# A two-layer-pair network on one core: each FFN begins with two plain column groups instead of one, and all phases share one pool of 2 KB weight tiles

## The chip, the core and the metric

The kernel runs on one core of a Trainium2 chip. Its five engines work side by side, each through its own queue in order: TensorE (PE, with its weight loads PEld), VectorE (DVE), ScalarE (ACT), GpSimd (POOL) and SyncE (SP), which here only issues transfers. The metric is device microseconds of one execution. The kernel before took 2481.24 us, the median of three runs between 2480.6 and 2482.82 us.

## The reference

A sequence of 512 positions of width 1024 goes through four layers, each a mixer and an FFN with residual additions: an mLSTM mixer, a windowed attention mixer, a parallel mixer (sparse attention beside a state-space branch) and a short convolution. All of it is float32. The part that matters here is the FFN, four times with weights of its own and D_FF = 2816:

```
def rmsnorm(x, w):
    xf = x.astype(jnp.float32)
    y = xf * lax.rsqrt(jnp.mean(xf * xf, axis=-1, keepdims=True) + EPS)
    return (y * w.astype(jnp.float32)).astype(x.dtype)

def swiglu(h, w_in, w_out):
    gu = h @ w_in
    gate, up = gu[..., :D_FF], gu[..., D_FF:]
    return (jax.nn.silu(gate) * up) @ w_out

x = x + swiglu(rmsnorm(x, norm_w), w_in, w_out)
```

## The kernel before

**Layout and arithmetic.** x lies transposed in eight tiles xT of 128 features by 512 positions. Every float32 product is made of three matmuls: each operand is split into a high part (whi, xh), which ScalarE rounds (`split`, L176; `hilo`, L232), and a low part (wlo, xl), the rest, which VectorE subtracts (`sub`, L164), and high x high, high x low and low x high are summed in one PSUM bank (`mm3`, L216 to L218). So each weight costs one pass of ScalarE and one of VectorE before TensorE can use it.

**The FFN.** The 2816 columns of gate and of up are worked through in 11 groups jj of 256 gate and 256 up columns. Group 0 is *plain* (`first`, L498): four blocks of 128 columns, 8 tiles of x each, 96 matmuls of 512 columns. The norm is folded in: the matmuls read x times the norm's weight (xh, xl from L289 and L290), and the row scale rb, which needs the sums of squares of all eight tiles (L282, L298, L255), multiplies the result when it is evacuated (L510). Groups 1 to 10 use a Strassen scheme (`seven`, L456): seven products of 24 matmuls with 256 columns, 168 in all, in the place of eight. It needs sums of weight blocks (S, L423 on GpSimd and L428 on VectorE) and four combinations of x (`combine`, L390, tiles thi and tlo). Products go to banks g, s, t and o (`seven`, L457); the third is the first that goes to t. After three or four groups the down projection adds to x (`out_part`).

**Banks.** `share` gives each tag its PSUM banks; in the FFN g has two, s three, t two and o one. The plain group asks for t, o, t, o (L505), and its norm uses s. The mixers' output projections (`add_out`, L333) use g and s, in the short convolution s and t.

**Weight buffers.** `wpool` (L1646) opens a pool for each phase: in a mixer 8 buffers of 2 KB a partition for high parts and as many for low ones, in an FFN 4 of 4 KB. With 4 KB a split covers 1024 elements a partition (4 tiles of x by 256 columns), with 2 KB 512. Raw weights come in 512 KB transfers into 5 buffers (`load_raw`, L181).

**What sets the order.** The program is written phase after phase, and a scheduler of the framework places each engine's instructions when the program is built, by the order of writing as a priority and by when it expects inputs and free buffers. In the text the first group's weights stand behind the norm.

The functions that the change touches, with what calls them:

## Time and profile before

| | before |
|---|---|
| median of three runs | 2481.24 us |
| the profiled execution | 2479.76 us, of which its span 2478.1 us |
| TensorE busy | 2388.4 us (96%), 14196 matmuls |
| VectorE busy | 1866.2 us (75%) |
| ScalarE busy | 1160.3 us (47%) |
| GpSimd busy | 437.2 us (18%) |
| granted TensorE clock, mean | 0.984 |
| read from HBM | 219.45 MB, 89 GB/s |

The granted clock is the share of 2.4 GHz that TensorE was given; it has two levels, 0.5 and 1.0 of that. A matmul's shown duration is longer than its distance to the next one, since matmuls are pipelined; how fast they run is read from their starts, or from how many fit in a stretch. The four FFNs begin at about 248, 830, 1576 and 2117 us of the span. A wait is put down to the instruction whose semaphore came last.

### The profile page before, as it was taken

The numbers are of one execution on the slowest core, as the hardware profiler recorded it, in microseconds if no ns is written. First come the engines' busy times: TensorE is split into PE (matmuls) and PEld (weight loads), VectorE is DVE, ScalarE is ACT, GpSimd is POOL, SyncE is SP. The second block draws the span as 40 slices with busy tenths as digits, with TensorE's granted clock in tenths as the row PEclk, the third lists the DMA queues.
The fourth block names the chain that finished last, engine by engine and source line by source line (L and its number), as shares of the span: only waits on it lengthen the run. The fifth ranks groups of instructions, "written<-read, shape, count | busy, mean of one in ns | idle before, by whom it ended". The sixth has DMA issues, their size and how long they took to land.

```text
span 2478.1 us, 36192 instructions
## 1 busy us (share of the span) xinstructions
PE 2388.4 (96%) x14196; PEld 2088.1 (84%) x14196; DVE 1866.2 (75%) x2826; ACT 1160.3 (47%) x1869; POOL 437.2 (18%) x318
## 2 busy tenths in 40 slices
PE   8999899999999899999999899899999999999998
PEld 7898799998767698989777777798989788899997
DVE  7677888787867786967889978876867755857777
ACT  4444544444577553534554455453534323545434
POOL 2210100000352100000456346100000010101100
PEclk9999999999989999999999999999999999999999
DMA  4331232323311132323221133222323332223232
GB/s 164 116 99 43 94 115 86 119 81 116 98 39 35 60 103 85 120 85 100 94 62 60 52 110 100 80 86 94 111 94 103 102 97 91 88 91 120 82 107 77
DMA packets 73434, 226.60 MB, mean 91 GB/s; under 512 B 10336, under 2 KB 14576, under 8 KB 73264
## 3 DMA queue, kind: packets, MB, share of 16 engines
q1 hardware_dynamic: 68896, 220.00, 26.8%
q10 hardware_dynamic: 4320, 4.21, 0.6%
q8 instruction: 111, 1.82, 0.3%
q14 instruction: 59, 0.48, 0.1%
q0 software_dynamic: 48, 0.10, 0.0%
HBM read 219.45 MB, written 2.20 MB: 89 GB/s over the span
## 4 chain that ended last, share of the span: by engine, by line
PE 82%; DVE 10%; DMA 2%; ACT 2%; issue 2%; POOL 1%; ACTq 0%; SPq 0%; DVEq 0%; POOLq 0%
PE ps_g L216 6%; PE ps_g L218 6%; PE ps_g L217 6%; PE ps_g L446 5%; PE ps_g L445 5%; PE ps_g L444 5%; PE ps_s L216 4%; PE ps_s L218 3%; PE ps_s L217 3%; PE ps_t L444 3%; PE ps_t L445 3%; PE ps_t L446 3%; PE ps_t L217 3%; PE ps_t L216 3%; PE ps_t L218 3%; DVE wlo L164 2%
## 5 line engine op out<-in xcount | busy, mean ns | idle before, releaser
L176 ACT ACTIVATE whi<-wraw 128x512 fp32r<-128x512 f32 (+1 forms) x488 | 394.7, 819 | 614.0 <-PE ps_g L217 195.8
L164 DVE TENSOR_TENSOR wlo<-wraw,whi 128x512 fp32r<-128x512 f32 (+1 forms) x428 | 441.1, 1040 | 173.2 <-ACT whi L176 164.3
L423 POOL TENSOR_TENSOR S<-wraw 128x1024 f32<-128x1024 f32 x40 | 117.0, 2924 | 1161.7 <-DMA wraw<-in_in_dram 995.1
L176 ACT ACTIVATE whi<-S 128x1024 fp32r<-128x1024 f32 x160 | 169.6, 1060 | 261.3 <-PE ps_g L445 115.5
L216 PE MATMUL ps_g<-xh,whi 128*128 128x512 f32 (+1 forms) x632 | 259.3, 410 | 14.0 <-DVE fa L1223 6.4
L164 DVE TENSOR_TENSOR wlo<-S,whi 128x1024 fp32r<-128x1024 f32 x160 | 209.2, 1308 | 76.2 <-ACT whi L176 76.2
L218 PE MATMUL ps_g<-xh,wlo 128*128 128x512 f32 (+1 forms) x632 | 254.8, 403 | 1.0 <-DVE wlo L164 1.0
L217 PE MATMUL ps_g<-xl,whi 128*128 128x512 f32 (+1 forms) x632 | 254.1, 402 | 0.0
L446 PE MATMUL ps_g<-thi,wlo 128*128 128x256 f32 x640 | 183.3, 286 | 5.5 <-DVE wlo L164 5.5
L444 PE MATMUL ps_g<-thi,whi 128*128 128x256 f32 x640 | 183.1, 286 | 3.7 <-ACT whi L176 3.7
L445 PE MATMUL ps_g<-tlo,whi 128*128 128x256 f32 x640 | 182.8, 286 | 0.0
L216 PEld LDWEIGHTS ps_g<-xh,whi 128*128 128x128 f32 (+1 forms) x632 | 121.8, 193 | 45.6 <-DVE fa L1223 7.5
L218 PEld LDWEIGHTS ps_g<-xh,wlo 128*128 128x128 f32 (+1 forms) x632 | 121.5, 192 | 29.5 <-issue 2.2
L217 PEld LDWEIGHTS ps_g<-xl,whi 128*128 128x128 f32 (+1 forms) x632 | 121.8, 193 | 25.2 <-issue 1.1
L446 PEld LDWEIGHTS ps_g<-thi,wlo 128*128 128x128 f32 x640 | 124.7, 195 | 6.3 <-DVE wlo L164 6.3
L444 PEld LDWEIGHTS ps_g<-thi,whi 128*128 128x128 f32 x640 | 124.5, 195 | 4.6 <-ACT whi L176 4.6
L445 PEld LDWEIGHTS ps_g<-tlo,whi 128*128 128x128 f32 x640 | 124.5, 195 | 0.0
L164 POOL TENSOR_TENSOR wlo<-wraw,whi 128x512 fp32r<-128x512 f32 (+1 forms) x60 | 79.6, 1336 | 142.0 <-ACT whi L176 96.2
L217 PE MATMUL ps_s<-hlo,whi 128*128 128x512 f32 x264 | 102.8, 389 | 0.0
L218 PE MATMUL ps_s<-hhi,wlo 128*128 128x512 f32 x264 | 102.7, 389 | 0.0
L216 PE MATMUL ps_t<-hhi,whi 128*128 128x512 f32 x264 | 102.7, 389 | 0.0
L217 PE MATMUL ps_t<-hlo,whi 128*128 128x512 f32 x264 | 102.7, 389 | 0.0
(564 smaller groups left out, 6980.0 us busy)
## 6 DMA issues: line engine op xcount, KB each, us to landing
wraw<-in_in_dram SPq DMA_DIRECT2D x176, 512.0 KB, 3.5
wraw<-in_down_dram SPq DMA_DIRECT2D x82, 512.0 KB, 3.5
wraw<-in_par_in_dram SPq DMA_DIRECT2D x30, 512.0 KB, 3.6
wraw<-in_mlstm_in_dram SPq DMA_DIRECT2D x24, 512.0 KB, 3.9
wraw<-in_sc_in_dram SPq DMA_DIRECT2D x24, 512.0 KB, 3.5
wraw<-in_attn_in_dram SPq DMA_DIRECT2D x12, 512.0 KB, 4.2
wraw<-in_par_out_dram SPq DMA_DIRECT2D x12, 512.0 KB, 5.9
mb<-drs SPq DMA_DIRECT2D x16, 256.0 KB, 3.6
```

The costliest lines, as they stand in the source:

```text
L164: (V if e == "V" else G).tensor_tensor(lo, x, hi.bitcast(F32), op=ALU.subtract)
L176: A.activation(hi, raw[:, k:k + st, :], AF.Copy)
L216: T.matmul(o, lhsT=w[0], rhs=x[0], start=start, stop=False)
L217: T.matmul(o, lhsT=w[0], rhs=x[1], start=False, stop=False)
L218: T.matmul(o, lhsT=w[1], rhs=x[0], start=False, stop=stop)
L423: G.tensor_tensor(live[jj, "S1"], live[jj, 2], live[jj, 3], op=ALU.add)
L444: T.matmul(o, lhsT=w[0], rhs=x[i][0], start=start and i == j == 0, stop=False, skip_group_check=True)
L445: T.matmul(o, lhsT=w[0], rhs=x[i][1], start=False, stop=False, skip_group_check=True)
L446: T.matmul(o, lhsT=w[1], rhs=x[i][0], start=False, stop=end, skip_group_check=True)
```

## The change

Each FFN now begins with two plain groups. `plain_weights` asks for a plain group's weights; the first group's stand ahead of the norm in the text, the second's behind the first group's matmuls. The first group goes to banks g, s, g, s, the second to t, o, t, o. The combinations of x are written after the first group's evacuation, and the Strassen runs begin with group 2. All phases take their weights from one pool with 8 buffers of 2 KB for high and 8 for low parts, so every split covers at most 512 elements, also in the Strassen products and in the down projections; the norm uses bank t. The gate weights of the mLSTM take their tiles from the same pool.

```
@@ -68,6 +68,7 @@
     sp = ctx.enter_context(tc.tile_pool(name="sp", bufs=2, **RIGHT))
     rp = ctx.enter_context(tc.tile_pool(name="rp", bufs=3, **RIGHT))
     xsp = ctx.enter_context(tc.tile_pool(name="xsp", bufs=8))
+    wp = ctx.enter_context(tc.tile_pool(name="wp", bufs=8))
     pp = ctx.enter_context(tc.tile_pool(name="pp", bufs=1, space=PSUM))
     dp = ctx.enter_context(tc.tile_pool(name="dp", bufs=1, space=bass.MemoryType.DRAM))
...
@@ -163,20 +165,12 @@
         e = lo_on[0][turn[0] % len(lo_on[0])]
         (V if e == "V" else G).tensor_tensor(lo, x, hi.bitcast(F32), op=ALU.subtract)
 
-    def weight_tile(tag, name, nk, n):
-        pool, bufs, _ = weight_pool
-        return pool.tile([P, nk, n], F32R, tag=tag, name=name, bufs=bufs)
-
     def split(raw, nk, n):
-
-        res = []
-        st = max(1, min(nk, weight_pool[2] // n))
-        for k in range(0, nk, st):
-            hi, lo = weight_tile("whi", "whi", st, n), weight_tile("wlo", "wlo", st, n)
-            A.activation(hi, raw[:, k:k + st, :], AF.Copy)
-            sub(lo, raw[:, k:k + st, :], hi)
-            res += [(hi[:, i, :], lo[:, i, :]) for i in range(st)]
-        return res
+        hi = wp.tile([P, nk, n], F32R, tag="whi", name="whi", bufs=WB)
+        lo = wp.tile([P, nk, n], F32R, tag="wlo", name="wlo", bufs=WB)
+        A.activation(hi, raw, AF.Copy)
+        sub(lo, raw, hi)
+        return [(hi[:, k, :], lo[:, k, :]) for k in range(nk)]
 
     def load_raw(w, k0, c0):
         rows, n, cw, mk = _W[w]
@@ -194,11 +188,6 @@
         for k in range(0, nk, 4):
             m = min(4, nk - k)
             raw = load_raw(w, k0 + k, c0)
-            if weight_pool[2] >= m * n:
-                w4 = split(raw, m, n)
-                for b in range(0, n, P):
-                    res[b // P] += [(hi[:, b:b + P], lo[:, b:b + P]) for hi, lo in w4]
-                continue
             for b in range(0, n, P):
                 res[b // P] += split(raw[:, :, b:b + P], m, P)
         return res
@@ -206,10 +195,11 @@
     def load_b(w, k0, nk, c0, n):
 
         res = []
-        mk = _W[w][3]
+        mk, st = _W[w][3], 512 // n
         for k in range(0, nk, mk):
             raw = load_raw(w, k0 + k, c0)
-            res += split(raw, mk, n)
+            for i in range(0, mk, st):
+                res += split(raw[:, i:i + st, :], st, n)
         return res
 
     def mm3(o, w, x, start, stop):
@@ -361,9 +351,20 @@
         V.tensor_tensor(xT[m], ps, xT[m], op=ALU.add)
 
 
+    def plain_weights(wi, jj):
+
+        ws = [], [], [], []
+        for k in (0, 4):
+            for n, c in enumerate((0, DFF)):
+                raw = load_raw(wi, k, c + jj * 256)
+                for i in range(2):
+                    ws[n + 2 * i].extend(split(raw[:, :, i * P:(i + 1) * P], 4, P))
+        return ws
+
     def ffn(L, last=False, aside=None):
         wi, wd = f"in{L}", f"down{L}"
-        xs = norm(f"ffn{L}", tag="s", later=True)
+        pending = plain_weights(wi, 0)
+        xs = norm(f"ffn{L}", later=True)
         parts = [(0, 3), (3, 6), (6, 9), (9, 11)] if last else [(0, 4), (4, 8), (8, 11)]
         hid = {}
         HS = slice(0, S // 2), slice(S // 2, S)
@@ -430,7 +431,7 @@
                     live[jj, "S2"] = t
             else:
                 t = {0: r[0], 1: r[1], 2: live[jj, "S1"], 6: r[3]}[s]
-            live[jj, "w", s] = split(t, 4, 256)
+            live[jj, "w", s] = [split(t[:, :, j * P:(j + 1) * P], 4, P) for j in range(2)]
 
         def product(jj, s, ps, start):
             ws = live.pop((jj, "w", s))
@@ -438,8 +439,7 @@
             for j in range(2):
                 o = ps[:, HS[j]]
                 for i in range(4):
-                    c = slice(j * P, (j + 1) * P)
-                    w = [t[:, c] for t in ws[i]]
+                    w = ws[j][i]
                     end = i == 3
                     T.matmul(o, lhsT=w[0], rhs=x[i][0], start=start and i == j == 0, stop=False, skip_group_check=True)
                     T.matmul(o, lhsT=w[0], rhs=x[i][1], start=False, stop=False, skip_group_check=True)
@@ -495,23 +495,22 @@
             for jj in jjs:
                 seven(jj, ahead)
 
-        def first():
-            ws = [], [], [], []
-            for k in (0, 4):
-                for n, c in enumerate((0, DFF)):
-                    for hi, lo in split(load_raw(wi, k, c), 4, 256):
-                        for i in range(2):
-                            ws[n + 2 * i].append([t[:, i * P:(i + 1) * P] for t in (hi, lo)])
-            pss = group_a(xs, ws, ["t", "o", "t", "o"], {4: xs.sums, 6: xs.rows})
-            for i in range(4):
-                combine(i)
+        def plain_evac(jj, pss):
             g, u = scr("fg", (P, 2, S)), scr("fu", (P, 2, S))
             for i in range(2):
                 V.tensor_tensor(g[:, i, :], pss[2 * i], xs.rb, op=ALU.mult)
             A.activation(g, g, AF.Silu)
             for i in range(2):
                 V.tensor_tensor(u[:, i, :], pss[2 * i + 1], g[:, i, :], op=ALU.mult)
-            store(0, u)
+            store(jj, u)
+
+        def first():
+            pss = group_a(xs, pending, ["g", "s", "g", "s"], {4: xs.sums, 6: xs.rows})
+            ws = plain_weights(wi, 1)
+            plain_evac(0, pss)
+            for i in range(4):
+                combine(i)
+            plain_evac(1, group_a(xs, ws, ["t", "o", "t", "o"]))
 
 
         def add_row(m, ps):
@@ -611,7 +610,7 @@
 
         first()
         for p, (a, b) in enumerate(parts):
-            run(range(max(a, 1), b))
+            run(range(max(a, 2), b))
             if last:
                 if p == 0:
                     xnat = to_nat()
...
@@ -1642,12 +1641,6 @@
     rope = ExitStack()
     TILE = dict(reuse_waits="tile")
 
-    @contextmanager
-    def wpool(name, bufs, width):
-        with tc.tile_pool(name=name, bufs=bufs, **TILE) as pool:
-            weight_pool[:] = pool, bufs, width
-            yield
-
     for n, L in enumerate(layers):
         last = n == len(layers) - 1
         if L == 1 and n == 0:
...
@@ -1668,7 +1661,7 @@
         if before_window:
             rope_pool[0] = rope.enter_context(tc.tile_pool(name="rope", bufs=1, **RIGHT))
         share(PB[4])
-        with wpool(f"wf{L}", 4, 1024), tc.tile_pool(name=f"tf{L}", bufs=4, **TILE) as hidden[1], \
+        with tc.tile_pool(name=f"tf{L}", bufs=4, **TILE) as hidden[1], \
                 tc.tile_pool(name=f"hf{L}", bufs=4, **TILE) as hidden[0], \
                 tc.tile_pool(name=f"ff{L}", bufs=2, **TILE) as phase[0]:
             ffn(L, last=last, aside=rope_tables if before_window else None)
```

In the order as built (an instruction's line is that of its own file: L164 of before is L166 now, L348 is L338, L290 is L280, L282 is L272, L510 is L501, L397 is L398) the change shows at three places, all at the beginning of FFN 0.

VectorE at the end of the mLSTM's output projection. xT is x, and its numbers are the eight tiles. Before:

```order
L348 TENSOR_TENSOR xT_106<-ps_g,xT_106 128x512
L348 TENSOR_TENSOR xT_107<-ps_s,xT_107 128x512
L348 TENSOR_TENSOR xT_108<-ps_g,xT_108 128x512
L348 TENSOR_TENSOR xT_109<-ps_s,xT_109 128x512
L290 SCALAR_TENSOR_TENSOR xl<-xT_106,cols,xh 128x512
L290 SCALAR_TENSOR_TENSOR xl<-xT_107,cols,xh 128x512
L282 TENSOR_TENSOR ssum<-ssum,sq 128x512
```

The same place now:

```order
L338 TENSOR_TENSOR xT_109<-ps_g,xT_109 128x512
L338 TENSOR_TENSOR xT_110<-ps_s,xT_110 128x512
L166 TENSOR_TENSOR wlo<-wraw,whi 128x512
L338 TENSOR_TENSOR xT_111<-ps_g,xT_111 128x512
L166 TENSOR_TENSOR wlo<-wraw,whi 128x512
L338 TENSOR_TENSOR xT_112<-ps_s,xT_112 128x512
L166 TENSOR_TENSOR wlo<-wraw,whi 128x512
L280 SCALAR_TENSOR_TENSOR xl<-xT_109,cols,xh 128x512
L166 TENSOR_TENSOR wlo<-wraw,whi 128x512
```

Low parts of weights have moved in between the residual additions, three of them ahead of the norm's first xl.

VectorE around the evacuation of the first plain group (fg and fu are its gate and up halves, S a sum of weight blocks). Before:

```order
L164 TENSOR_TENSOR wlo<-S,whi 128x1024
L510 TENSOR_TENSOR fg<-ps_t,rb 128x512 x2
L465 TENSOR_TENSOR fg<-ps_s,pc 128x2x256
L428 TENSOR_TENSOR S<-S,wraw 128x1024
L513 TENSOR_TENSOR fu<-ps_o,fg 128x512
```

And now:

```order
L166 TENSOR_TENSOR wlo<-wraw,whi 128x512 x4
L501 TENSOR_TENSOR fg<-ps_g,rb 128x512 x2
L504 TENSOR_TENSOR fu<-ps_s,fg 128x512 x2
L398 TENSOR_TENSOR fu<-S 128x512
L166 TENSOR_TENSOR wlo<-wraw,whi 128x512 x2
L400 TENSOR_TENSOR fu<-S,fu 128x256
L223 TENSOR_TENSOR hlo<-fu,hhi 128x1024
```

Before, the evacuation stands behind low parts of Strassen weights, with a Strassen product's result (L465) right after it; now it stands behind the second plain group's weights, and the first combination of x (L398) comes after it.

TensorE at the end of the first plain group. Before:

```order
L216 MATMUL ps_t<-xh,whi 128x512
L217 MATMUL ps_t<-xl,whi 128x512
L218 MATMUL ps_t<-xh,wlo 128x512
L444 MATMUL ps_g<-xh,whi 128x256
L445 MATMUL ps_g<-xl,whi 128x256
L446 MATMUL ps_g<-xh,wlo 128x256
```

And now:

```order
L206 MATMUL ps_g<-xh,whi 128x512
L207 MATMUL ps_g<-xl,whi 128x512
L208 MATMUL ps_g<-xh,wlo 128x512
L206 MATMUL ps_s<-xh,whi 128x512
L207 MATMUL ps_s<-xl,whi 128x512
L208 MATMUL ps_s<-xh,wlo 128x512
L206 MATMUL ps_t<-xh,whi 128x512
L207 MATMUL ps_t<-xl,whi 128x512
L208 MATMUL ps_t<-xh,wlo 128x512
L206 MATMUL ps_o<-xh,whi 128x512
```

Where the first Strassen product followed the plain group, the second plain group follows now, in other banks. The order of SP's transfers is the same in both but for one pair of small transfers in the parallel mixer.

## Rows read from the trace of the kernel before

**Rows 1.** the page's first part: busy time, share of the span, instructions.

```profile
PE 2388.4 (96%) x14196; PEld 2088.1 (84%) x14196; DVE 1866.2 (75%) x2826; ACT 1160.3 (47%) x1869; POOL 437.2 (18%) x318
```

**Rows 2.** windows, Strassen run and mixer: stretch, length, busy (count) by engine.

```profile
400.00:460.00 60.00, 60.00 (x503) 60.00 (x502) 53.20 (x49) 33.13 (x39) 7.11 (x2) 1.00 0.33 107
1980.00:2040.00 60.00, 60.00 (x266) 49.68 (x265) 31.13 (x48) 15.81 (x25) 5.88 (x4) 1.00 0.31 97
```

**Rows 3.** windows at the beginnings of the four FFNs, columns as above.

```profile
245.00:300.00 55.00, 46.44 (x261) 40.51 (x260) 43.90 (x63) 27.85 (x33) 9.41 (x2) 0.94 0.22 77
827.00:882.00 55.00, 47.70 (x266) 41.77 (x265) 43.46 (x64) 28.37 (x34) 9.15 (x2) 0.94 0.21 77
1573.00:1640.00 67.00, 57.12 (x335) 50.97 (x335) 57.47 (x78) 38.44 (x47) 5.82 (x2) 0.92 0.25 86
2115.00:2160.00 45.00, 42.86 (x256) 37.38 (x255) 37.97 (x50) 22.45 (x26) 7.82 (x2) 1.00 0.27 94
```

**Rows 4.** the same windows, L216's matmuls alone: length, PE busy (count), clock.

```profile
245.00:300.00 55.00, 13.96 (x36) 0.94 0.22 77
827.00:882.00 55.00, 14.14 (x36) 0.94 0.21 77
1573.00:1640.00 67.00, 14.23 (x36) 0.92 0.25 86
2115.00:2160.00 45.00, 13.66 (x35) 1.00 0.27 94
```

**Rows 5.** TensorE's waits in the whole span: us in total, times, longest.

```profile
PE ps_t L444 <- DVE fg L510: 8.3, 3, 3.7
PE ps_g L216 <- DVE fa L1223: 6.4, 3, 3.8
PE ps_g L446 <- DVE wlo L164: 5.5, 4, 3.2
PE ps_t L1042 <- ACT rd L1062: 3.9, 1, 3.9
```

**Rows 6.** TensorE's timeline in FFN 0: start, us, what [idle before <-releaser].

```profile
283.72 0.58 PE L444 MATMUL ps_t<-thi,whi 128*128 128x256 f32 x1 [3.71 <-DVE fg L510]
284.10 0.41 PE L445 MATMUL ps_t<-tlo,whi 128*128 128x256 f32 x1
284.31 0.41 PE L446 MATMUL ps_t<-thi,wlo 128*128 128x256 f32 x1
```

**Rows 7.** the chain of waits, 245 to 300 us: start, us, what.

```profile
257.98 7.07 POOL S L423
```

**Rows 8.** VectorE's timeline in a Strassen run, columns as in rows 6.

```profile
408.02 0.68 DVE L476 TENSOR_TENSOR fu<-ps_g,pc 128x512 f32<-128x512 f32 x1
408.62 0.68 DVE L478 TENSOR_TENSOR fu<-ps_o,pc 128x512 f32<-128x512 f32 x1
411.48 1.22 DVE L479 TENSOR_TENSOR fu<-fu,fg 128x1024 f32<-128x1024 f32 x1
412.62 1.22 DVE L164 TENSOR_TENSOR wlo<-S,whi 128x1024 fp32r<-128x1024 f32 x1
417.17 2.89 DVE L164 TENSOR_TENSOR wlo<-wraw,whi 128x1024 fp32r<-128x1024 f32 x1 [0.46 <-ACT whi L176]
```

**Rows 9.** timeline ahead of FFN 0: first residual addition, first FFN matmul.

```profile
235.32 0.69 DVE L348 TENSOR_TENSOR xT<-ps_g,xT 128x512 f32<-128x512 f32 x1 [1.45 <-PE ps_g L218]
248.38 0.50 PE L216 MATMUL ps_t<-xh,whi 128*128 128x512 f32 x1 [0.86 <-ACT whi L176]
```

**Rows 10.** VectorE's groups by shape: count | busy us, mean ns | idle.

```profile
L164 DVE TENSOR_TENSOR wlo<-wraw,whi 128x1024 fp32r<-128x1024 f32 x218 | 283.2, 1306 | 116.3 <-ACT whi L176 115.5
L164 DVE TENSOR_TENSOR wlo<-wraw,whi 128x512 fp32r<-128x512 f32 x210 | 158.1, 764 | 56.9 <-ACT whi L176 48.8 <-PE ps_t L255 7.2 <-PE ps_g L218 0.5
```

**Rows 11.** VectorE's waits, 400 to 460 us, columns as in rows 5.

```profile
DVE wlo L164 <- ACT whi L176: 4.6, 6, 1.7
DVE fg L471 <- PE ps_t L446: 0.9, 1, 0.9
```

More of the change, by code (lines that the diff above doesn't have):

```diff
@@ L1 @@
-from contextlib import ExitStack, contextmanager
+from contextlib import ExitStack
 import numpy as np
@@ L91, in tile_net @@
     hidden = [None, None]
-    weight_pool = [None, 0, 0]
     def hid_tile(tag, bufs, dt=F32R):
@@ L102, in scr @@
         return pool.tile(list(shape), dt, tag=tag, name=tag, bufs=bufs)
+    WB = 8
     RB = 5
@@ L638, in mlstm @@
         for k in (0, 4):
-            hi = weight_tile("whi", "ghi", 4, P)
-            lo = weight_tile("wlo", "glo", 4, P)
+            hi = wp.tile([P, 4, P], F32R, tag="whi", name="ghi", bufs=WB)
+            lo = wp.tile([P, 4, P], F32R, tag="wlo", name="glo", bufs=WB)
             G.memset(hi.bitcast(F32), 0.0)
@@ L1658, in tile_net @@
         if L == 2:
-            with wpool(f"wm{L}", 8, 512), tc.tile_pool(name=f"hm{L}", bufs=8) as hidden[0]:
+            with tc.tile_pool(name=f"hm{L}", bufs=8) as hidden[0]:
                 parallel(n > 0)
         else:
-            with wpool(f"wm{L}", 8, 512), tc.tile_pool(name=f"hm{L}", bufs=8) as hidden[0], \
+            with tc.tile_pool(name=f"hm{L}", bufs=8) as hidden[0], \
                     tc.tile_pool(name=f"mix{L}", bufs=2) as phase[0]:
```

## The prediction, made before the changed kernel ran

> **What bounds the kernel now.** I read the page's first part, then the busy time of stretches, then the waits, and only then the timeline, because a share over the whole span mixes stages with different limits. TensorE is busy 96% of the span, VectorE 75% [rows 1]. Two stretches show what TensorE costs when nothing holds it up: 503 matmuls of 256 columns in 60 us inside a Strassen run, 0.1193 us each, and 266 matmuls of 512 columns in 60 us, 0.2256 us each [rows 2]. Inside the Strassen runs and the down projections TensorE is 60.00 of 60 busy at full clock; a change there can win only by taking matmuls away.
>
> The loss is at the four places where an FFN begins. Four windows each begin with the last 12 matmuls of the mixer's output projection and end when the second Strassen group is under way [rows 3]. Of their matmuls, three times the L216 count have 512 columns [rows 4], 12 are the small ones of the norm (taken here as 0.12 us each, an estimate from the 256-column matmul), the rest have 256. FFN 0: 108 x 0.2256 + 141 x 0.1193 + 1.4 = 42.6 of 55 us, so 12.4 us lost. FFN 1: 108 and 146 make 43.2 of 55, lost 11.8. FFN 2: 108 and 215 make 51.4 of 67, lost 15.6. FFN 3: 105 and 139 make 41.7 of 45, lost 3.3. Together 43.1 us, 1.7% of the span, and it is what a change of the FFN's beginning can reach.
>
> Who ends these waits: the largest, 8.3 us in three waits, is the Strassen product into bank t that waits for L510, the evacuation of the plain group that sat in the same bank; next come waits for VectorE's low halves of the weights, 5.5 us [rows 5]. The timeline shows the rest of the price: TensorE starts at 283.72 after 3.71 us of idle time, and its matmuls then stand 0.21 us apart where 0.12 is normal [rows 6]; the granted clock of the window is 0.94 [rows 3], which is a few us at the lower of the two levels, 1.2 GHz. 24 matmuls at 0.09 us more are 2.2 us. The chain of waits in the same window runs over VectorE and a 7.07 us sum on GpSimd [rows 7], not over transfers: at an FFN's start VectorE (43.90 of 55 us busy [rows 3]) has the residual additions, the norm, all four combinations of x for Strassen, and the split weights, and the only plain group gives TensorE 21.7 us to hide them behind.
>
> **The change part by part.**
>
> *A second plain group in place of a Strassen group.* 96 x 0.2256 = 21.65 us against 168 x 0.1193 = 20.04 us [rows 2]: +1.61 us in each FFN, +6.4 us in all. This is certain, since TensorE is the bound there.
>
> *What the second group hides.* TensorE then has 43.3 us of plain work before the first Strassen product. VectorE's work in that time, at the spacing of its starts, 0.60 us for 512 elements and 1.14 for 1024 [rows 8]: 8 residual additions 4.8, 8 xl 5.3 (at 0.66, an estimate a tenth over 0.60), 7 sums of squares 4.2, 16 half-size low parts of plain weights 9.6, the norm's small ones 2.3 (estimate), evacuating the first group 2.4 and its low half 1.1, four combinations with their low halves 9.7, the first four Strassen low parts 2.4: 41.8 us. It begins, as before, 13 us ahead of the FFN's first matmul, while the projection still runs [rows 9]. So 41.8 us of VectorE stand against 56 us of TensorE, where before some 35 us (the same list without the second group's share and the first group's evacuation, which had to wait) stood against the same 13 us and 21.7. The evacuation of the first group no longer stands in the Strassen product's way, since that group lies in banks g and s and the second lies between. I therefore let the 43.1 us go, and ask what is late next: the second plain group is still evacuated from t, and the third Strassen product needs t and the fourth combination. That costs two evacuations and one low half, 2 x 0.60 + 1.14 = 2.3 us, in FFN 0 to 2 and one low half, 1.1 us, in FFN 3: 8 us left. Its bounds are 0 (all of it behind the two products into g and s, 5.8 us) and the whole wait as it is today, 8.3 us of idle time plus three stretches at the lower clock, 14.9 us more than forecast.
>
> *Weights asked for ahead of the norm.* Four low parts now stand between the residual additions on VectorE, 4 x 0.60 = 2.4 us, so the norm's first xl comes 2.4 us later; the first matmul that reads it is 13 us behind the first addition [rows 9], so I count nothing. It takes away the two waits at the first plain matmuls, already in the 43.1. All eight weight buffers may still be held by the projection; then part of those two waits, about 2 us an FFN, comes back. SP's queue keeps its order, so no transfer moves past another.
>
> *Banks g and s for the first group.* The projection has just used them, so the last of four blocks waits for the last residual addition; that addition feeds the norm's last xl anyway. I count 0, at most one addition, 0.6 us, in each FFN.
>
> *2 KB weight tiles everywhere.* A split of 1024 elements becomes two of 512: 2 x 0.60 - 1.14 = 0.06 us more on VectorE by starts [rows 8], or 2 x 0.764 - 1.306 = 0.22 us by mean durations [rows 10]. A Strassen group has 7 splits: 0.4 to 1.6 us more per 20.04 us. VectorE is busy 53.20 of 60 us there [rows 2], 17.8 us a group; 18.2 to 19.3 fit. I take the lower end, as the durations overlap their successors, and cost it at nothing: what hides it is VectorE's own idle time of 5.5 us in 60 [rows 11].
> The Trainium skill ("Perfetto Trace Analysis", section "Optimizing Scalar/DVE Operations") puts some 60 ns of access overhead on each VectorE instruction and says that larger operations help when the engine is saturated. Its figure gives the same 0.4 us a group as the starts do; by its rule the split costs time only from saturation on, which is the slower rival below, and 53.20 of 60 says not yet.
>
> *The mixers.* Their tiles and counts stay, but the scheduler interleaves the window and the parallel mixer anew. One long wait more or less in each is the bound I give it, 3.8 and 3.9 us [rows 5]: +-8 us, taken as 0.
>
> Sum on the profiled execution, whose span of 2478.1 lies in 2479.76 us: 2479.8 - 43.1 + 6.4 + 8 = 2451.1. The median of the runs, 2481.24, lies 1.5 us above it, so the forecast is 2452.5.
>
> **Rivals.** *The wait for t stays.* The second group's evacuation replaces the first's: VectorE, in order, reaches it behind combinations, and the third Strassen product is late just as now. For it: the banks t and o are the same, and o is a single bank. Against it: the row scale is long known by then, and two products lie in front. Price 14.9 us: 2467.
>
> *VectorE becomes the bound in the Strassen runs (slower).* Place: the 36 groups left. 17.8 us busy plus 1.6 by durations plus the 1.8 us a group in which VectorE waits for ScalarE's high part or a product [rows 11], if those waits stay because each half split waits again: 21.2 against 20.04, 1.1 us a group, 40 us, so 2492. It decides from 20.04 us a group on, and makes the kernel slower than before from 0.8 us over. For it: one split that started at 417.17 took 2.89 us, as if something held VectorE up [rows 8]. Against it: that one is already in the 53.20, and waits shrink when work fills them.
>
> *More goes than forecast.* Nothing is left at the FFN starts and the mixers gain a wait: 2452.5 - 8 - 4 = 2440.
>
> *The mixers give it back in part*, one long wait each plus the weight waits of the projection: 2452.5 + 8 + 6 = 2466.
>
> **How the numbers follow.** Forecast (2444 to 2460) 0.62, wait for t 0.14, mixers 0.06, more gained 0.06, VectorE the bound 0.12. The predicted time is 2452. The range of 2440 to 2474 takes in all but the slow rival and some of the edges. A change under 0.2%, 5 us, can't be told from none here. Faster 0.88; the slow rival with its lower prices gives 0.03 of no change and 0.09 of slower.
>
> **What would show it.** Right: at the four FFN starts no wait of TensorE over 3 us, a granted clock of 1.00, and 43 us of plain matmuls without a hole before the first Strassen product; 384 more 512-column matmuls and 672 fewer of 256. The half splits start 0.60 us apart and VectorE stays below 19.3 us a Strassen group. Wrong: TensorE's share below 60 of 60 inside a Strassen run with the waits put down to VectorE's low parts, or a wait of over 3 us at the third Strassen product for the second group's evacuation.

## The result and the profile after

The changed kernel takes 2452.8 us (median of 4 runs, 2451.14 to 2453.84), the kernel before 2481.6 in the same series: a ratio of 0.9883, 95% interval 0.9866 to 0.9900. The forecast was 2452. The profiled run took 2452.76 us with a span of 2451.0. The time is right and so is most of the way to it, but the step on what is late next was not, and the errors of the sum nearly cancel. One of seven executions of experiment 2 took 4782.31 us and is left out of its median below.

The page's first part, as in [rows 1]:

```profile
PE 2382.7 (97%) x13908; PEld 2072.2 (85%) x13908; DVE 1866.8 (76%) x3172; ACT 1205.6 (49%) x2219; POOL 428.0 (17%) x314
```

288 matmuls fewer: 384 more of 512 columns, 672 fewer of 256, as forecast. VectorE has 346 instructions more and the same busy time. The same four windows as [rows 3], then L206 alone (L216 before) as [rows 4], with its weight loads beside TensorE's busy time:

```profile
245.00:300.00 55.00, 53.28 (x271) 45.10 (x269) 41.80 (x72) 28.36 (x43) 2.63 (x1) 1.00 0.20 60
827.00:882.00 55.00, 53.93 (x328) 48.08 (x327) 46.34 (x71) 28.77 (x43) 5.13 (x2) 1.00 0.24 77
1573.00:1640.00 67.00, 63.49 (x386) 56.80 (x385) 53.54 (x83) 34.34 (x51) 5.61 (x2) 0.95 0.26 79
2115.00:2160.00 45.00, 45.00 (x279) 40.64 (x278) 40.09 (x58) 26.24 (x39) 2.46 (x1) 1.00 0.35 106
...
245.00:300.00 55.00, 24.79 (x64) 11.90 (x64) 1.00 0.20 60
```

Before, TensorE was busy 46.44, 47.70, 57.12 and 42.86 us in these windows [rows 3]. The clock is now 1.00 in three windows and 0.95 in FFN 2. By the count of the prediction FFN 0 now does 192 x 0.2256 + 67 x 0.1193 + 1.4 = 52.7 us of work in 55; 12.4 us were lost there, 2.3 are now.

The largest waits of TensorE in the span, as in [rows 5]; the wait for t behind L510 (now L501) is gone from the list, the mixers' remain:

```profile
PE ps_g L206 <- DVE fa L1222: 5.4, 3, 4.7
PE ps_s L155 <- POOL ident masks.py:199: 5.0, 1, 5.0
PE ps_t L245 <- DVE nrc L298: 4.4, 1, 4.4
PE ps_s L943 <- issue: 3.9, 1, 3.9
```

What is left stands in FFN 2. Its TensorE timeline (start, length, what, idle time before):

```profile
1603.96 0.28 PE L445 MATMUL ps_t<-tlo,whi 128*128 128x256 f32 x1
1604.92 0.39 PE L446 MATMUL ps_t<-thi,wlo 128*128 128x256 f32 x1 [0.68 <-DVE wlo L166]
...
1607.71 0.58 PE L444 MATMUL ps_g<-thi,whi 128*128 128x256 f32 x1 [1.92 <-ACT whi L171]
...
1608.72 0.58 PE L445 MATMUL ps_t<-tlo,whi 128*128 128x256 f32 x1 [0.21 <-DVE tlo L223]
...
1610.15 0.58 PE L444 MATMUL ps_t<-thi,whi 128*128 128x256 f32 x1 [0.63 <-ACT thi L222]
...
1611.18 0.41 PE L444 MATMUL ps_g<-thi,whi 128*128 128x256 f32 x1
1611.39 0.41 PE L445 MATMUL ps_g<-tlo,whi 128*128 128x256 f32 x1
```

TensorE waits for halves of weights and of combinations, 3.4 us in all and not for an evacuation, and its matmuls then stand 0.21 us apart where 0.12 is normal: the lower of the two clock levels, as in FFN 0 before [rows 6].

To compare kernels I use one measure from the timelines: the time from an FFN's first matmul to the first matmul of its down projection. With two plain groups and two Strassen groups it is 192 x 0.2256 + 336 x 0.1193 = 83.4 us of work, and the shortest measured is 85.2 (FFN 3, with one Strassen group: 65.1); with one plain group 1.6 less. "Lost" is the sum of what lies above these, worked out from the rounded figures and good to some 0.2 us. In experiment 2, 24 projection matmuls that are mixed into FFN 0 and FFN 1 are taken out (5.4 us each) and counted with the mixers. "Mixers" is the time from the program's start, or the last matmul of an FFN, to the next FFN's first matmul, summed over the four. Experiment 8 changes the Strassen groups themselves and has no row.

| kernel | ratio to before | FFN 0, 1, 2, 3 (us) | lost | mixers |
|---|---|---|---|---|
| before | 1 | 95.2, 94.3, 97.5, 66.9 | 39.7 | 1048.0 |
| after | 0.9883 | 87.7, 87.1, 92.5, 65.2 | 11.8 | 1042.2 |
| 1 one group | 1.0159 | 105.5, 102.5, 104.0, 81.8 | 79.6 | 1050.9 |
| 2 first group in t, o | 0.9966 | 92.3, 92.3, 92.2, 66.1 | 22.2 | 1048.2 |
| 3 combinations first | 0.9839 | 85.2, 85.2, 85.2, 65.1 | 0 | 1037.1 |
| 4 three groups in FFN 2 | 0.9879 | 87.8, 87.1, 88.1, 65.2 | 5.9 | 1042.6 |
| 5 = 3 with one group | 0.9936 | 91.3, 91.4, 97.6, 63.4 | 29.5 | 1039.7 |
| 6 before, 2 KB tiles | 1.0029 | 90.1, 90.2, 95.3, 68.0 | 29.4 | 1066.9 |
| 7 before, second group | 1.0019 | 95.1, 94.2, 97.1, 70.2 | 35.9 | 1049.9 |
| 9 before, group and banks | 0.9894 | 86.6, 86.1, 86.7, 65.5 | 4.2 | 1051.3 |
| 10 = 3 again | 0.9828 | 85.2, 85.2, 85.2, 65.1 | 0 | 1037.3 |
| 11 = 3, FFN 3 with one group | 0.9820 | 85.2, 85.2, 85.2, 63.4 | 0 | 1044.2 |
| 12 = 3, pools by phase | 0.9894 | 86.1, 86.1, 86.6, 65.9 | 4.0 | 1054.9 |

Before to after: 39.7 - 11.8 = 27.9 us no longer lost, 6.4 paid for dearer matmuls, 5.8 gained in the mixers: 27.3, against 27.1 between the spans.

Every row of the table is one execution. The FFN segments repeat: FFN 0, 1 and 2 are 85.2 us each in experiments 3, 10 and 11, and FFN 0, 1 and 3 agree within 0.1 us between the changed kernel and experiment 4. The mixers do not: experiments 10 and 11 have the same instructions up to FFN 3, and their mixers differ by 6.9 us. So a difference of up to 7 us in that column is not shown to come from an edit. Of the 5.8 here, 3.3 are seen: before, TensorE waits 0.86, 0.92 and 1.53 us for its first weights ahead of FFN 0, 1 and 2 (the first of them in [rows 9]), and after the change it doesn't.

### The profile page after: what moved, and what is told of

It reads as the page before. It is cut to its first block, busy times and chain, and to the rows that moved or that the text cites. A ratio compares the mean times of both kernels' runs of the same rounds, so it can differ in the third digit from the quotient of the medians.

```text
span 2451.0 us, 36810 instructions
## 1 busy us (share of the span) xinstructions
PE 2382.7 (97%) x13908; PEld 2072.2 (85%) x13908; DVE 1866.8 (76%) x3172; ACT 1205.6 (49%) x2219; POOL 428.0 (17%) x314
## 4 chain that ended last, share of the span: by engine, by line
PE 61%; DVE 8%; ACT 1%; issue 1%; DMA 1%; POOL 0%; ACTq 0%; DVEq 0%
PE ps_g L206 4%; PE ps_g L207 4%; PE ps_g L208 4%; PE ps_g L446 3%; PE ps_g L444 3%; PE ps_g L445 3%; PE ps_s L206 3%; PE ps_s L208 3%; PE ps_s L207 3%; PE ps_t L207 2%; PE ps_t L206 2%; PE ps_t L208 2%; PE ps_t L446 2%; PE ps_t L445 2%; PE ps_t L444 2%; PE ps_o L446 1%
## 5 line engine op out<-in xcount | busy, mean ns | idle before, releaser
L171 ACT ACTIVATE whi<-wraw 128x512 fp32r<-128x512 f32 (+1 forms) x726 | 447.6, 621 | 670.6 <-PE ps_g L207 237.0
L166 DVE TENSOR_TENSOR wlo<-wraw,whi 128x512 fp32r<-128x512 f32 x666 | 487.8, 743 | 186.5 <-ACT whi L171 173.8
L424 POOL TENSOR_TENSOR S<-wraw 128x1024 f32<-128x1024 f32 x36 | 104.0, 2889 | 1146.8 <-DMA wraw<-in_in_dram 794.2
L206 PE MATMUL ps_g<-xh,whi 128*128 128x512 f32 (+1 forms) x696 | 283.6, 409 | 9.2 <-DVE fa L1222 5.2
L207 PE MATMUL ps_g<-xl,whi 128*128 128x512 f32 (+1 forms) x696 | 279.8, 402 | 0.0
L208 PE MATMUL ps_g<-xh,wlo 128*128 128x512 f32 (+1 forms) x696 | 279.3, 402 | 0.0
L171 ACT ACTIVATE whi<-S 128x512 fp32r<-128x512 f32 x288 | 178.1, 628 | 191.0 <-PE ps_g L445 59.0
L166 DVE TENSOR_TENSOR wlo<-S,whi 128x512 fp32r<-128x512 f32 x288 | 202.7, 730 | 35.0 <-ACT whi L171 33.2
L206 PEld LDWEIGHTS ps_g<-xh,whi 128*128 128x128 f32 (+1 forms) x696 | 134.0, 193 | 40.8 <-DVE fa L1222 5.8
L444 PE MATMUL ps_g<-thi,whi 128*128 128x256 f32 x576 | 163.8, 284 | 2.7 <-ACT whi L171 1.9
L446 PE MATMUL ps_g<-thi,wlo 128*128 128x256 f32 x576 | 163.7, 284 | 0.2
L445 PE MATMUL ps_g<-tlo,whi 128*128 128x256 f32 x576 | 163.4, 284 | 0.0
L166 POOL TENSOR_TENSOR wlo<-wraw,whi 128x512 fp32r<-128x512 f32 (+1 forms) x60 | 83.2, 1397 | 139.2 <-ACT whi L171 124.2
L206 PE MATMUL ps_t<-hhi,whi 128*128 128x512 f32 x264 | 102.7, 389 | 0.0
```

Of the source, the lines that this page charges most:

```text
L166: (V if e == "V" else G).tensor_tensor(lo, x, hi.bitcast(F32), op=ALU.subtract)
L171: A.activation(hi, raw, AF.Copy)
L206: T.matmul(o, lhsT=w[0], rhs=x[0], start=start, stop=False)
L207: T.matmul(o, lhsT=w[0], rhs=x[1], start=False, stop=False)
L208: T.matmul(o, lhsT=w[1], rhs=x[0], start=False, stop=stop)
L424: G.tensor_tensor(live[jj, "S1"], live[jj, 2], live[jj, 3], op=ALU.add)
```

## The experiments

The ratios go with the runs of the kernel before on the same chip, whose median was 2479 to 2480 us in all four series.

**1. One group.** From the changed kernel:

```diff
-            ws = plain_weights(wi, 1)
             plain_evac(0, pss)
...
-            plain_evac(1, group_a(xs, ws, ["t", "o", "t", "o"]))
...
-            run(range(max(a, 2), b))
+            run(range(max(a, 1), b))
```

> The changed kernel with the second plain group taken out again: group 0 stays in banks g and s, its weights stay ahead of the norm, the tiles stay 2 KB. Theory A (the second group is what hides VectorE's work at an FFN's start): the 6.4 us of dearer matmuls go and at least 25 of the some 31 us that the starts had gained come back, 2452.8 - 6.4 + 25 = 2471 us (2465 to 2478), with TensorE waits for VectorE ahead of the first Strassen products. Theory B (the banks and the early weights did it, the second group only costs): 2452.8 - 6.4 = 2446 us (to 2451).

Measured: 2517.3 us, ratio 1.0159 (1.0143 to 1.0175). Theory A holds in sign and is far short in size: not 25 us came back but 68 (from 11.8 lost to 79.6). TensorE's waits in its FFN 0, then VectorE's there (us in total, times, longest):

```profile
PE ps_t L444 <- ACT whi L171: 10.6, 1, 10.6
...
DVE fg L501 <- ACT rb L246: 5.5, 1, 5.5
DVE nv L288 <- PE ps_t L239: 4.3, 1, 4.3
DVE ssum L272 <- ACT sq L271: 2.6, 3, 1.2
DVE fu L504 <- ACT fg L502: 2.5, 1, 2.5
```

In these four rows VectorE waits 14.9 us of the 55 from 245 to 300 us. It is not short of time, it works in order: L501, the evacuation, waits for rb, the norm's row of scales, and everything behind it waits along. ScalarE, in order as well, shows how that reaches TensorE:

```profile
282.68 2.00 ACT L222 ACTIVATE thi<-fu 128x1024 fp32r<-128x1024 f32 x2 [2.80 <-DVE fu L401]
285.25 1.15 ACT L171 ACTIVATE whi<-S 128x512 fp32r<-128x512 f32 x2 [0.57 <-POOL S L424]
```

The high half that TensorE waits 10.6 us for comes behind high halves of combinations that waited for VectorE. That makes the order of evacuation and combinations (experiment 3) the suspect.

**2. The first group back in t and o.** From the changed kernel:

```diff
-        xs = norm(f"ffn{L}", later=True)
+        xs = norm(f"ffn{L}", tag="s", later=True)
...
-            pss = group_a(xs, pending, ["g", "s", "g", "s"], {4: xs.sums, 6: xs.rows})
+            pss = group_a(xs, pending, ["t", "o", "t", "o"], {4: xs.sums, 6: xs.rows})
```

> The changed kernel with its first plain group back in banks t and o (the norm's small sums in s, as before the change); both plain groups then use the same banks. Theory A (cover by matmuls is the main thing): only the evacuation of group 0 stands in the way of group 1, some 2.4 us of VectorE and a few matmuls at the lower clock in each FFN, 2456 to 2462 us. Theory B (banks of their own are the main thing): the 8.3 us of waits for t come back, now ahead of group 1, with half clock behind them: 2467 us or more.

Measured: 2470.9 us, ratio 0.9966 (0.9954 to 0.9977), B by the time; at the starts 10.4 us more are lost, between the two, and 6.0 us more stand in the mixers, no more than two executions of the same mixers differ by. Its TensorE in FFN 0:

```profile
265.67 1.11 PE L245 MATMUL ps_s<-ident,nrc 128*128 128x128 f32 x4 [2.66 <-DVE nrc L234]
268.20 0.79 PE L206 MATMUL ps_t<-xh,whi 128*128 128x512 f32 x1 [1.41 <-DVE fg L501]
```

The second group cannot begin before the first is out of t, and that waits for the scales (nrc). 4.1 us of idle time, and FFN 0 loses 7.1: the rest passes at the lower clock (the clock is 0.94 from 244 to 300 us).

**3. Combinations first.** From the changed kernel, the order in the text that the kernel before had:

```diff
             ws = plain_weights(wi, 1)
-            plain_evac(0, pss)
             for i in range(4):
                 combine(i)
+            plain_evac(0, pss)
```

> The changed kernel with the four combinations written ahead of the first group's evacuation, as they were before the change. Theory A: nothing needs banks g and s before the first Strassen product, 21.65 us later, and the sum of VectorE's work is the same: 2453 us (2450 to 2456). Rival: VectorE's order is what counts (the evacuation early, the combinations late), and putting it back costs a wait for g or s at the first Strassen product, 2 to 4 us in each FFN: 2460 us or more.

Measured: 2438.7 us, ratio 0.9839 (0.9822 to 0.9856); again 2437.7, 0.9828 (0.9813 to 0.9842). Both expectations are wrong: neither had a gain, and all that was left at the starts went, 11.8 us; the medians lie 14.1 us apart, the mixers of the two profiled executions 5. The interval lies below that of the change, so this version beats both kernels. VectorE in FFN 0, first in the changed kernel, then in the repeated run of this one (start, length, what, idle time before):

```profile
264.01 0.16 DVE L288 TENSOR_SCALAR nv<-ps_t 128x4 f32<-128x4 f32 x1 [4.27 <-PE ps_t L239]
...
272.45 1.29 DVE L501 TENSOR_TENSOR fg<-ps_g,rb 128x512 f32<-128x512 f32 x2 [1.29 <-ACT rb L246]
276.21 1.29 DVE L504 TENSOR_TENSOR fu<-ps_s,fg 128x512 f32<-128x512 f32 x2 [2.46 <-ACT fg L502]
277.41 0.68 DVE L398 TENSOR_TENSOR fu<-S 128x512 f32<-128x512 f32 x1
```

```profile
245.10 0.68 DVE L398 TENSOR_TENSOR fu<-S 128x512 f32<-128x512 f32 x1
...
263.83 1.22 DVE L223 TENSOR_TENSOR tlo<-fu,thi 128x1024 fp32r<-128x1024 f32 x1
270.44 0.16 DVE L288 TENSOR_SCALAR nv<-ps_t 128x4 f32<-128x4 f32 x1 [1.93 <-PE ps_t L239]
...
280.25 1.29 DVE L501 TENSOR_TENSOR fg<-ps_g,rb 128x512 f32<-128x512 f32 x2
```

Behind the evacuation the first combination starts at 277.41; ahead of it at 245.10, in the holes between the norm's steps, and the last one's low half starts at 263.83. The evacuation starts 8 us later, and nobody waits, since the second group stands in other banks. TensorE in this FFN 0 and FFN 2 (columns as in [rows 2]):

```profile
243.00:300.00 57.00, 57.00 (x297) 48.98 (x296) 51.00 (x81) 31.93 (x48) 5.11 (x2) 1.00 0.26 84
1573.00:1640.00 67.00, 67.00 (x457) 62.38 (x457) 56.91 (x81) 36.23 (x55) 5.23 (x2) 1.00 0.34 111
```

**4. A third group in FFN 2.** From the changed kernel: in FFN 2 groups in t, o, then g, s, then t, o.

```diff
+            order = [["t", "o", "t", "o"]] * three + [["g", "s", "g", "s"]]
+            for jj, banks in enumerate(order):
+                pss = group_a(xs, ws, banks, {} if jj else {4: xs.sums, 6: xs.rows})
+                ws = plain_weights(wi, jj + 1)
+                plain_evac(jj, pss)
...
+            run(range(max(a, 3 if three else 2), b))
```

> The changed kernel with a third plain group in FFN 2 alone, where 7.9 us are still lost (banks t and o, then g and s, then t and o). Theory A (VectorE's work of the FFN's start is still more than two groups hide there): the 7.9 us fall to 1 or less for 1.6 us of dearer matmuls: 2446.5 us (2444 to 2450). Rival: what is late there is the preparing of the Strassen weights itself (difference, high half, low half), which moves along with the first product: nothing gained, 1.6 us paid, 2454 us (2452 to 2457).

Measured: 2448.9 us, ratio 0.9879 (0.9862 to 0.9896). In FFN 2, 92.5 became 88.1, of which 86.8 can't be avoided with three groups: theory A, as far as the segment goes (1.3 us are left, where 1 or less was expected). The interval overlaps that of the change, so the whole time doesn't show it. It buys cover where experiment 3 needs none.

**5. Experiment 3 with one group.** The lines of experiment 1, taken out of experiment 3.

> One plain group in banks g and s, with the combinations ahead of its evacuation as in the kernel before; 2 KB tiles and weights ahead of the norm as in the changed kernel. It is the run of 2438.66 us (combinations first) without its second group. Theory A (one group hides too little of VectorE's work, in whatever order): 6.4 us of dearer matmuls go, 15 to 30 us are lost again at the four starts: 2455 us (2447 to 2462). Rival (banks of their own and the combinations first suffice, the second group only costs): 2438.7 - 6.4 = 2432 us (2430 to 2437).

Measured: 2463.9 us, ratio 0.9936 (0.9922 to 0.9950): theory A, 1.9 us above its range. The second group is worth some 25 us here. Without it 29.5 us are lost, as much as with the tiles alone (experiment 6): with one group the banks of its own, the earlier weights and the one pool together add nothing at the starts. TensorE's idle times in its FFN 0:

```profile
272.39 0.36 PE L444 MATMUL ps_t<-thi,whi 128*128 128x256 f32 x1 [1.25 <-DVE nv L288]
...
277.56 0.65 PE L245 MATMUL ps_t<-ident,nrc 128*128 128x128 f32 x4 [2.05 <-DVE nrc L234]
...
279.62 0.58 PE L444 MATMUL ps_g<-xh,whi 128*128 128x256 f32 x1 [1.41 <-DVE fg L501]
```

All three end on the chain of the norm's scales: nv, nrc, and then the evacuation of g. That chain is what the second group hides. In FFN 3 one group loses nothing (63.4).

**6. The tiles alone.** From the kernel before:

```diff
-        with wpool(f"wf{L}", 4, 1024), tc.tile_pool(name=f"tf{L}", bufs=4, **TILE) as hidden[1], \
+        with wpool(f"wf{L}", 8, 512), tc.tile_pool(name=f"tf{L}", bufs=4, **TILE) as hidden[1], \
```

> The kernel before with its FFN weight pool of four 4 KB buffers turned into eight of 2 KB, nothing else. Theory: the tiles neither cost nor gain by themselves, 2479 us (2475 to 2484). Rival (buffers that come free in halves are part of the gain at the starts): 2470 us or less. Rival from the prediction (the split lows load VectorE until it is the bound in the Strassen runs): 2490 us or more.

Measured: 2487.2 us, ratio 1.0029 (1.0017 to 1.0040). Neither theory nor rival: the starts lose 10 us less, the mixers, of which no line was changed, take 19 us more.

**7. The second group alone.** From the kernel before; its combinations stay ahead of the evacuations.

```diff
+            ws = plain_weights(1)
             for i in range(4):
                 combine(i)
+            plain_evac(0, pss)
+            plain_evac(1, group_a(xs, ws, ["t", "o", "t", "o"]))
...
-            run(range(max(a, 1), b))
+            run(range(max(a, 2), b))
```

> The kernel before with a second plain group, nothing else: both groups in banks t and o, 4 KB tiles, weights behind the norm, the combinations ahead of both evacuations. Theory that cover and banks are both needed: the second group waits in t for an evacuation that stands behind 9.7 us of combinations, so the wait of before is only moved; 2471 us as with the banks undone, plus up to 5 us a start: 2480 us (2468 to 2492). Rival (the second group alone does it): 2455 us or less.

Measured: 2484.8 us, ratio 1.0019 (1.0008 to 1.0029). As the theory said: the wait for t moves from the third Strassen product to the second group, and 6.4 us are paid for 3.8 us less lost. TensorE's largest waits in its FFN 0 (us in total, times, longest):

```profile
PE ps_s L255 <- DVE nrc L244: 3.5, 1, 3.5
PE ps_t L216 <- DVE fg L510: 1.4, 1, 1.4
```

**8. VectorE loaded.** From the changed kernel, the first low half of each of the seven steps computed twice:

```diff
         sub(lo, raw, hi)
+        if again:
+            V.tensor_tensor(lo, raw, hi.bitcast(F32), op=ALU.subtract)
```

> The changed kernel with the first low half of each of the seven steps of every Strassen group computed twice, seven more VectorE instructions of 512 elements a group, 7 x 0.60 = 4.2 us. VectorE is busy 53.30 of 60 us there, 17.8 us a group of 20.04. Theory (busy time by the profile is VectorE's real load): 22.0 us against 20.04, 2.0 us x 36 groups = 70 us: 2523 us (2500 to 2540), and TensorE waits for low halves inside the runs. Rival (much of the busy time is waiting for ports or semaphores, so there is more room than shown): 2460 us or less.

Measured: 2485.0 us, ratio 1.0014 (1.0005 to 1.0023), 32 us above the change where 70 were expected, and neither theory nor rival by the time. Its windows in a run of four groups and the down projection behind it, then TensorE's waits from 400 to 460 us:

```profile
400.00:420.00 20.00, 20.00 (x169) 20.00 (x169) 20.00 (x27) 12.44 (x21) 3.29 (x1) 1.00 0.29 99
420.00:440.00 20.00, 19.61 (x164) 19.40 (x162) 20.00 (x29) 10.44 (x18) 3.74 (x1) 1.00 0.25 81
440.00:460.00 20.00, 17.72 (x141) 16.91 (x141) 20.00 (x28) 11.40 (x19) 0.15 (x1) 1.00 0.34 107
460.00:480.00 20.00, 20.00 (x112) 17.52 (x112) 13.46 (x20) 8.30 (x12) 0.00 (x0) 1.00 0.47 158
...
PE ps_t L448 <- DVE wlo L174: 1.4, 1, 1.4
PE ps_o L448 <- DVE wlo L174: 0.5, 1, 0.5
PE ps_g L448 <- DVE wlo L174: 0.4, 1, 0.4
```

VectorE is busy 20.00 of 20 and TensorE still loses only 2.7 us in 60. So the load is real, since TensorE now waits for low halves, but a run is at most four groups long, and VectorE recovers in the down projection (13.46 of 20 us busy); that it also enters the run with weights prepared is my reading, not shown by these rows. My price per group was one for a run without end.

**9. Second group and banks, without the rest.** Experiment 7 with the first group in g and s and the norm's small sums in t (the two lines of experiment 2, the other way round); 4 KB tiles, pools by phase.

> The kernel before with a second plain group and with banks g and s for the first one (the norm's small sums in t); the 4 KB tiles, the weights behind the norm and the combinations ahead of the evacuations stay as in the kernel before. Theory (the second group and the banks together are the whole gain, tiles and early weights count nothing): the time of the changed kernel with combinations first, 0.984 of before, 2441 us (2434 to 2448), and 85 us from an FFN's first matmul to its down projection in FFN 0 to 2. Rival (2 KB tiles come free sooner and take some 10 us at the starts): 2450 us or more, 87 to 90 us each.

Measured: 2454.2 us, ratio 0.9894 (0.9880 to 0.9907). By the total the rival, by the segments neither: 86.6 us and not 87 to 90, only 4.2 us lost. Of the 18.0 us between its profiled span (2452.2) and that of experiment 3 repeated (2434.2), 14.0 are in the mixers; the medians lie 16.5 us apart.

**10 and 11. Experiment 3 again, and with one group in FFN 3.**

```diff
-            plain_evac(1, group_a(xs, ws, ["t", "o", "t", "o"]))
+            if not last:
+                plain_evac(1, group_a(xs, ws, ["t", "o", "t", "o"]))
```

> The changed kernel with the combinations written ahead of the first evacuation, once more, as the measure for the two runs beside it: 0.984 of before, 2437 to 2444 us.

> The combinations-first kernel with one plain group instead of two in FFN 3 alone, where one group lost only 1.7 us. Theory: 1.6 us of dearer matmuls go there and nothing else: 1.6 us under the combinations-first kernel beside it, 63.4 us instead of 65.1 from FFN 3's first matmul to its down projection. Rival: the work around it is interleaved anew and moves the time by more than that, up to 6 us either way.

Measured: 2437.7 and 2435.8 us, ratios 0.9828 and 0.9820 (0.9806 to 0.9833). FFN 3 is 1.6 us shorter, as expected; the totals can't be told apart.

**12. The pool split up again.** From experiment 3: a pool of eight 2 KB buffers for each mixer and each FFN.

```diff
-    wp = ctx.enter_context(tc.tile_pool(name="wp", bufs=8))
+    wpl = [None]
...
-            with tc.tile_pool(name=f"hm{L}", bufs=8) as hidden[0], \
+            with tc.tile_pool(name=f"wm{L}", bufs=8, **TILE) as wpl[0], tc.tile_pool(name=f"hm{L}", bufs=8) as hidden[0], \
...
-        with tc.tile_pool(name=f"tf{L}", bufs=4, **TILE) as hidden[1], \
+        with tc.tile_pool(name=f"wf{L}", bufs=8, **TILE) as wpl[0], tc.tile_pool(name=f"tf{L}", bufs=4, **TILE) as hidden[1], \
```

> The combinations-first kernel with the one weight pool split up again into one pool for each mixer and each FFN, as before the change, each of eight 2 KB buffers; groups, banks and order stay. Theory (the one pool over all phases is what makes the window mixer some 8 us shorter in all kernels that have it): 0.984 of before becomes 0.987 to 0.990, 2446 to 2455 us, with 226 us instead of 219 for the window mixer and 85.2 us still from an FFN's first matmul to its down projection. Rival (the size of the tiles or chance decides the mixers): 2434 to 2443 us.

Measured: 2455.3 us, ratio 0.9894 (0.9877 to 0.9911): the theory, except that the starts give 4 us as well. The medians of experiments 10 and 12 lie 17.6 us apart. Their profiled executions lie 21.5 us apart, 17.6 of that in the mixers and 4.0 at the starts, so the mixers' true share is nearer to 14 than to 17.6 (an estimate: 17.6 between the medians less 4.0). The window mixer in experiment 10, in this one and in experiment 11 (columns as in [rows 2]):

```profile
591.29:810.62 219.33, 205.62 (x975) 155.94 (x974) 163.66 (x378) 146.59 (x365) 72.84 (x67) 0.97 0.20 61
```

```profile
595.50:821.55 226.05, 210.99 (x975) 158.80 (x973) 167.37 (x380) 145.26 (x366) 72.88 (x67) 0.95 0.19 59
```

```profile
592.47:816.69 224.22, 212.15 (x974) 160.66 (x973) 162.46 (x378) 146.20 (x365) 73.46 (x67) 0.93 0.20 59
```

With the pool split up TensorE is busy 5.4 us longer at a clock of 0.95 instead of 0.97. But experiment 11 has the one pool and the instructions of experiment 10 here, and it too is busy 6.5 us longer, at 0.93: one execution can't show that the pool sets the clock. Over all runs the window mixer takes 217.6 to 224.2 us in the nine with the one pool (in experiment 2 with its 24 matmuls counted in) and 226.0 to 229.5 in the five with pools by phase. That the pool shortens it is shown by this and by the medians; why is open. The split pools also carry an option of the framework, `reuse_waits`, that the one pool lacks; the program as built has the same order of instructions without it, so the order comes from the split. Which buffer's release moves the work wasn't found. At the starts the 4 us go with the pools by phase as well: experiment 9 loses 4.2 with tiles of 4 KB, this one 4.0 with tiles of 2 KB.

## Why the prediction was right, and where not

*What the change can reach.* Right: the loss sat at the four starts, 43.1 us by my windows, 39.7 by the segments, and the change took away 27.9. Of what I had said would show it, no wait over 3 us is left at a start, the counts of matmuls agree, and the clock is 1.00 in three of the four windows. The 43 us of plain matmuls in a row did not come: in FFN 0 the first Strassen product starts 39.5 us after the first matmul (247.15 to 286.62), and the second group's last block, which needs the single bank o again, comes behind it, from 296.92.

*The second group's price*, 6.4 us: right. Where nothing is lost, FFN 3 takes 65.1 us with two groups and 63.4 with one.

*What the second group hides.* Right that it hides the start, and that it needs banks of its own. With the combinations first, the starts lose 39.7 us before, 35.9 with the group alone (7), 29.4 with the tiles alone (6), 29.5 with tiles and banks (5), 4.2 with group and banks (9), 0 with all (3). Wrong in the reason: I set 41.8 us of VectorE's work against 56 of TensorE, a question of load. What the starts wait for is a chain, from the sum of squares over the scales and rb to the evacuation. In the changed kernel the evacuation begins at 272.45, 25.3 us after the FFN's first matmul at 247.15; one group lasts 21.7. VectorE meanwhile has idle time.

*"What is late next"*, 8 us for the evacuation of the second group from t. This step failed in its mechanism and by 3.8 us in size. 11.8 us were left, 7.3 of them in FFN 2, and TensorE's waits for the second group's evacuation came to 0.2 us in FFN 0 and 0.4 in FFN 1, for bank o and none for t. Late were the halves of Strassen weights and combinations, since the combinations stood behind an evacuation that waits for rb. The diff shows that move, and I added up VectorE's work without asking when each piece could begin. Experiment 3, which undoes the move, loses nothing.

*Weights ahead of the norm*, counted 0: right. Written behind the norm, the changed program has the same order of instructions on every engine, so that no run could tell the two apart; it was not their place in the text that moved the low parts in between the residual additions. The waits for the first weights, which I put down to it, are gone.

*Banks g and s*, counted as a cost of 0 to 0.6 us: no wait for them shows at the starts. Their worth stood in my sum only as the evacuation that is out of the way; without them 10.4 us more are lost at the starts (experiment 2).

*2 KB tiles*, counted 0. Right for the Strassen runs: the halves start 0.60 us apart, and VectorE, with more and smaller splits, is busy no more than in [rows 2], 17.8 us a group. The same stretch of the changed kernel, then two of its splits and their successor:

```profile
400.00:460.00 60.00, 60.00 (x499) 59.83 (x498) 53.30 (x71) 37.23 (x60) 8.48 (x2) 1.00 0.34 116
...
411.80 1.28 DVE L166 TENSOR_TENSOR wlo<-wraw,whi 128x512 fp32r<-128x512 f32 x2
413.00 1.21 DVE L429 TENSOR_TENSOR S<-wraw,S 128x1024 f32<-128x1024 f32 x1
```

At the starts of the kernel before they took 10 us away, which I had not counted, and its mixers gave back more (experiment 6). The rule of the Trainium skill that I weighed here ("Perfetto Trace Analysis", section "Optimizing Scalar/DVE Operations"), that larger operations help a saturated engine, was not put to the test here, with VectorE busy 53.30 of 60 us.

*The mixers and the one pool*, taken as 0 with a bound of 8. In the profiled executions they gave 2.5 us beside the 3.3 of the waits for weights, inside the bound and less than two executions differ by. The one pool had no term of its own in my sum, and should have had: with combinations first it is worth 17.6 us by the medians, 4.0 of them at the starts (experiment 12). How much of that the change itself has is open.

*The rivals.* The wait for t stayed where the group or the banks were missing, not here. My price for it was added up wrongly: the whole wait of before, 14.9 us, would have come in the place of the 8 us already in the sum and not on top of them, 2459 and not 2467. VectorE was not the bound; 4.2 us more a group cost 32 us in all, not the 70 of my arithmetic, so that the price of 40 us I gave that rival was probably too high as well.

The mechanism held in the main, but that the sum came out within 2 us is luck, since its errors nearly cancel. The 43.1 us were right: 39.7 lie in the segments and 3.3 in the waits for weights ahead of them, which the change takes away as forecast. 3.8 us more were left than the 8, and the mixers gave 2.5. That makes +1.3 of the 1.7 us between the 2451.1 of the sum and the profiled 2452.8.

## What to carry to other kernels

Where an engine that works in order has an instruction that waits for a long chain, what is written behind it is late by the whole chain, however little work there is; add up not only its load but when its first instruction can begin. Cover and a place to put it, here a second group and banks of its own, gain only together. A pool that spans phases can change the time of phases in which no line was edited, so compare those segments by themselves, and over more than one execution.

## What the runs showed of the hardware

A wait of TensorE cost about twice its length where the clock fell behind it: 3.4 us of waits in FFN 2 of the changed kernel stand for 7.3 us lost, 4.1 in FFN 0 of experiment 2 for 7.1. And an engine at its limit need not cost what its overload says: VectorE busy 20.00 of 20 us in three stretches running cost TensorE 2.7 us.
